# Attention scores as three products of 64 rows, for the two halves of each head pair side by side

## The chip, the cores and the metric

One core of one Trainium2 chip. The metric is the device time of one execution in microseconds. An engine runs its own instructions in the order in which the program lists them: TensorE multiplies matrices into PSUM banks, VectorE and ScalarE work elementwise, and SyncE's queue issues most DMA transfers.

## The reference

Two layers over 256 latent and 256 context tokens of width 2048, in float32. The first layer mixes by a long convolution and a state space model. The second, which the change is in, is differential attention: 16 heads, and each has two halves of 64 channels with a softmax of their own.

```python
q_l = rope_2d(rms_norm(qk_shape(q_l, n_lat), q_norm))   # 16 heads, 2 halves, 64 channels
k_l = rope_2d(rms_norm(qk_shape(k_l, n_lat), k_norm))
...
s = jnp.einsum('bqhmd,bkhmd->bhmqk', q, k) * (DA_HEAD ** -0.5)
p = jax.nn.softmax(s, axis=-1)
w = p[:, :, 0] - lam * p[:, :, 1]
return jnp.einsum('bhqk,bkhe->bqhe', w, v)
```

The last layer makes queries for the 256 latent tokens only; keys and values come from all 512 tokens.

## The kernel before

Products that need precision are made from a high and a low part of each operand in fp32r: the cast (ScalarE) gives the high part, a subtraction (VectorE) the low one. A projection adds three products, high by high, high by low and low by high (lines 108 to 110). Its weights come through SyncE in pieces of 128x1024, three deep (`weights`), and are split the same way (lines 174 and 175).

The second layer runs over four chunks `c` of four heads. For each chunk:

- `project_rows` makes the queries (two token tiles), the keys (four) and the values (four). It goes over the 16 blocks of the inner dimension in pieces of two, and in each piece over up to four PSUM banks: two of the tag `acc` and two of the tag `aux`. Every tag has two banks.
- `heads` takes one finished bank of queries or keys: it norms (lines 1154 to 1160, at high priority; line 1160 is the last to read the bank), scales and rotates (1163 to 1173), transposes four times into a bank of the tag `tp` (1177), and calls `dst`, which is `queries` or `keys`. Then channels stand in rows: 64 rows for the first half of the head, 64 for the second.
- `keys` stacks for each half the high part in that half's own 64 rows and the low part in the other 64 (lines 1186 and 1187). `queries` puts the high part into both groups of 64 rows of one tile, and the low part into both of another (lines 1197 and 1199). So one product over 128 rows gives high by high plus high by low, and a second one the two with the low part of the query.
- For each head and each of two query tiles of 128 tokens: for each half `m`, a bank of the tag `wk`, two products of 128 rows and 512 columns (line 1259), the maximum (1260) and the exponential (1262), which is the last to read the bank. Then the weights are combined and transposed (1270, 1271), and later multiplied with the values into another `wk` bank (1277), normed (line 1283 is the last to read that bank) and transposed (1284). A projection for the gate (line 1248) comes ahead of each head; steps of the last gates (`last_gates`, products of 128 rows and 32 columns in line 580) come behind it.

The order of the instructions on each engine is not the order of the code. A planner goes through the program with costs of its own: an engine takes, of the instructions that are ready in the planner's time, the one that stands first in the code (or has high priority). An instruction that touches a new tile is ready once a buffer of its tag is free. So TensorE has products of the next projection between those of a head. The order is then fixed, and on the chip each engine waits at its semaphores in that order.

Names in the trace: `k` and `q` are the key and query tiles, `ps_wk`, `ps_acc`, `ps_aux` and `ps_tp` the banks, `prob` the weights, `s5HG`, `s5W`, `s5T` and `s5U` tiles of the first layer, where products of 64 rows and 64 columns (line 483) stand beside products of 128 rows and 64 columns (line 479).

Of the kernel before, what the change touches and what calls it, by code (L numbers as in the profile page):

```python
# [10 lines left out]
F32 = mybir.dt.float32  # L11
F32R = mybir.dt.float32r
# [3 lines left out]
MULT, ADD, SUB = ALU.mult, ALU.add, ALU.subtract  # L16
# [479 lines left out]
def hybrid_kernel(ctx: ExitStack, tc: tile.TileContext, A, out):  # L496
    nc = tc.nc
    v, act, pe, dma = nc.vector, nc.scalar, nc.tensor, nc.sync
# [3 lines left out]
    k = K(tc, main, psum)  # L502
# [194 lines left out]
    def project_rows(W, col, h, toks, done):  # L697
        bs = [k.bank("acc" if i < 2 else "aux") for i in range(len(toks))]
        rows(W, col, h, toks, bs, 0, len(h))
        for b, t in zip(bs, toks):  # L700
            done(t, b)
# [46 lines left out]
    W_in = A["ev_in_w"][0]  # L748
# [26 lines left out]
    with phase("start"):  # L775
# [13 lines left out]
        for i, w in enumerate((w1, w2)):  # L789
            b = k.bank("wk")  # L790
            pe.matmul(b[:64, :256], w, prev, start=True, stop=True)
            z = k.t([64, 256], "hyz")
# [33 lines left out]
        x = x_tiles()  # L826
# [56 lines left out]
        h = []  # L883
# [266 lines left out]
    def heads(i, tl, b, dst, t0):  # L1150

        with tc.high_priority():
            sq = k.e([128, 512], "qt", bufs=QT)
            act.activation(sq, b, AF.Square)
            r = k.e([128, 8], "qr", bufs=2)
            v.tensor_reduce(r, sq.rearrange("p (h j) -> p h j", h=8), axis=mybir.AxisListType.X, op=ADD)
            v.tensor_scalar(r, r, 1.0 / 64.0, EPS, op0=MULT, op1=ADD)
            r = rsqrt(k, r, [128, 8], "qrs")
            x = k.e([128, 8, 64], "qt", bufs=QT)
            v.tensor_tensor(x, b.rearrange("p (h j) -> p h j", h=8), r[:, :, None].to_broadcast([128, 8, 64]), op=MULT)  # L1160
        y = k.e([128, 8, 64], "qt", bufs=QT)
        if tl is None:
            v.tensor_tensor(y, x, nw[:, i][:, None, :].to_broadcast([128, 8, 64]), op=MULT)
        else:
            v.tensor_tensor(y, x, tab[:, i, 0, tl][:, None, :].to_broadcast([128, 8, 64]), op=MULT)
            z = sq.rearrange("p (h j) -> p h j", h=8)
            z4, x4 = (a.rearrange("p h (a z j) -> p (h a) z j", a=2, z=2) for a in (z, x))
            s4 = tab[:, i, 1, tl].rearrange("p (a z j) -> p a z j", a=2, z=2)
            for e in range(2):
                v.tensor_tensor(z.rearrange("p h (a z j) -> p h a z j", a=2, z=2)[:, :, :, e],  # L1170
                                x.rearrange("p h (a z j) -> p h a z j", a=2, z=2)[:, :, :, 1 - e],
                                s4[:, :, e][:, None].to_broadcast([128, 8, 2, 16]), op=MULT)
            v.tensor_tensor(y, y, z, op=ADD)
        tb = k.bank("tp", [128, 4, 128])
        yf = y.rearrange("p h j -> p (h j)")
        for c in range(4):
            pe.transpose(tb[:, c], yf[:, c * 128:c * 128 + 128], ident)
        dst(tb, t0)

    def keys(K):  # L1180

        def put(tb, t0):
            for m in range(2):
                s, o = slice(64 * m, 64 * m + 64), slice(64 - 64 * m, 128 - 64 * m)
                hi = K[m][s, :, t0:t0 + 128]
                act.copy(hi, tb[s])
                v.tensor_tensor(K[m][o, :, t0:t0 + 128], tb[s], hi.bitcast(F32), op=SUB)
        return put

    def queries(Q):  # L1190

        def put(tb, t0):
            for m in range(2):
                s, o = slice(64 * m, 64 * m + 64), slice(64 - 64 * m, 128 - 64 * m)
                hi, lo = (Q[m][z][:, :, t0:t0 + 128] for z in range(2))
                for p in (s, o):
                    act.copy(hi[p], tb[s])
                for p in (s, o):
                    v.tensor_tensor(lo[p], tb[s], hi[s].bitcast(F32), op=SUB)
        return put  # L1200

    with phase("mix"):
# [34 lines left out]
    with phase("attention"):  # L1237
        hl = [x[1] for x in h]
        om = []
        for c in range(4):  # L1240
            kT = [k.t([128, 4, 512], n, F32R) for n in ("k0", "k1")]
            qT = [[f([128, 4, 256], f"q{m}{z}", F32R) for z in range(2)] for m, f in enumerate((k.e, k.t))]
            vt = k.t([128, 4, 512], "vt", bufs=1)
            project_rows(W_in, c * 512, h, (2, 3), lambda t, b: heads(0, t - 2, b, queries(qT), (t - 2) * 128))
            project_rows(W_in, 2048 + c * 512, h, range(4), lambda t, b: heads(1, None if t < 2 else t - 2, b, keys(kT), t * 128))
            project_rows(W_in, 4096 + c * 512, h, range(4), lambda t, b: act.copy(vt[:, t], b))
            for hd in range(4):
                b = project(W_in, 6144 + (c * 4 + hd) * 128, hl, 0, 256)
                gt = k.t([128, 256], "gt", bufs=GT)
                act.activation(gt, b[:, :256], AF.Silu)  # L1250
                wT = [k.t([128, 4, 128], "wT", bufs=WT) for _ in range(2)]
                for qt in range(2):
                    z = k.t([128, 2], "z", bufs=4)
                    mx = k.t([128, 2], "mx", bufs=4)
                    ps = []
                    for m in range(2):
                        b = k.bank("wk")
                        for part in range(2):
                            pe.matmul(b, qT[m][part][:, hd, qt * 128:qt * 128 + 128], kT[m][:, hd], start=part == 0, stop=part == 1)  # L1259
                        v.tensor_reduce(mx[:, m:m + 1], b, axis=mybir.AxisListType.X, op=ALU.max, negate=True)  # L1260
                        p = k.t([128, 512], "prob", bufs=4)
                        act.activation(p, b, AF.Exp, bias=mx[:, m:m + 1], accum_out=z[:, m:m + 1])
                        ps.append(p)
                    v.reciprocal(z, z)
                    v.tensor_scalar(z[:, 1:2], z[:, 1:2], nlam, None, op0=MULT)
                    v.tensor_scalar(ps[0], ps[0], z[:, 0:1], None, op0=MULT)
                    v.scalar_tensor_tensor(ps[0], ps[1], z[:, 1:2], ps[0], op0=MULT, op1=ADD)
                    tb = k.bank("tp", [128, 4, 128])
                    for t in range(4):
                        pe.transpose(tb[:, t], ps[0][:, t * 128:t * 128 + 128], ident)  # L1270
                    act.copy(wT[qt], tb)
                ob = k.bank("tp")
                for qt in range(2):
                    qs = slice(qt * 128, qt * 128 + 128)
                    b = k.bank("wk")
                    for t in range(4):
                        pe.matmul(b[:, :128], wT[qt][:, t], vt[:, t, hd * 128:hd * 128 + 128], start=t == 0, stop=t == 3)  # L1277
                    o2 = k.t([128, 128], "o2", bufs=2)
                    r = k.t([128, 1], "or", bufs=2)
                    act.activation(o2, b[:, :128], AF.Square, accum_out=r)  # L1280
                    v.tensor_scalar(r, r, 1.0 / 128.0, EPS, op0=MULT, op1=ADD)
                    r = rsqrt(k, r, [128, 1], "ors")
                    v.tensor_scalar(o2, b[:, :128], r, None, op0=MULT)
                    pe.transpose(ob[:, qs], o2, ident)
                o = k.t([128, 256], "og", bufs=2)
                v.scalar_tensor_tensor(o, ob[:, :256], sw, gt, op0=MULT, op1=MULT)
                om.append([None, halves(o, k.m, "hlo")])
                next(rest)

        def residual(n, t, b):  # L1290
            g, xt = gate(1, 0, n, "prob", 4), k.t([128, 512], "prob", bufs=4)
            dma.dma_start(xt, x1scr[t - 2, n])
            v.tensor_tensor(g, b, g, op=MULT)
            v.tensor_tensor(g, g, xt, op=ADD)
            dma.dma_start(out[0, t * 128 - 256:t * 128 - 128, n * 512:n * 512 + 512], g)

        run(rest)
        W_out = A["od_out_w"][0]
        for n0 in (0, 2):
            bs = [[k.bank(tag) for _ in range(2)] for tag in ("acc", "aux")]  # L1300
            for k0, k1 in ((0, 12), (12, 16)) if n0 == 0 else ((0, 16),):
                for i in range(2):
                    rows(W_out, (n0 + i) * 512, om, (2, 3), bs[i], k0, k1)
                    if k1 == 16:
                        for j in range(2):
                            residual(n0 + i, 2 + j, bs[i][j])
# [29 lines left out]
```

## Time and profile before

| what | value |
|---|---|
| median of 3 runs | 1941.38 us (1938.76 to 1941.87) |
| the profiled execution | 1941.88 us |
| its span | 1939.7 us |
| TensorE busy | 1856.1 us (96%), 12607 products |
| weight loads busy | 1463.5 us (75%) |
| VectorE busy | 1286.6 us (66%) |
| ScalarE busy | 794.5 us (41%) |
| mean HBM traffic | 179 GB/s |

The span is the time from the first to the last instruction on the chip. PE is TensorE's products, PEld its weight loads, DVE is VectorE and ACT is ScalarE. The ends of products are modelled, and products overlap: the pace of a row of products is read from their starts. The attention stage runs from about 1215 us; scores are made in four stretches, 1310 to 1379, 1474 to 1543, 1638 to 1707 and 1802 to 1875 us.

### The profile page before, as it was taken

What the parts mean: (1) busy time and instruction counts of PE and PEld (TensorE: products, weight loads), DVE (VectorE), ACT (ScalarE), POOL (GpSimd) and SP (SyncE); (2) the same over time, 40 slices, a digit from 0 to 9 for tenths busy, and PEclk for the clock granted to TensorE, in tenths of its full rate; (3) what the DMA queues carried; (4) which work ended last, traced back from release to release, by engine and by line L of the source; (5) the groups of instructions that cost most, each with busy time, mean ns of one, the idle gap of its engine ahead of it and who ended that gap; (6) DMA issues with size and microseconds to landing.
All of it is one profiled execution on the core that took longest, in us unless ns stands there. A gap on an engine that the chain in (4) does not pass through costs nothing.

```text
span 1939.7 us, 31835 instructions
## 1 busy us (share of the span) xinstructions
PE 1856.1 (96%) x12607; PEld 1463.5 (75%) x12607; DVE 1286.6 (66%) x2497; ACT 794.5 (41%) x1252; POOL 6.9 (0%) x23
## 2 busy tenths in 40 slices
PE   3799989999999999999999999999999999999999
PEld 2677767777777677777788887778878878887877
DVE  3876677998997477368564347656765864666675
ACT  2442232322332333223342247437636734753762
POOL 0000000000000000000000000000000000000000
PEclk9899999999999999999999999999999999999999
DMA  8877656576774577655656355336335325523557
GB/s 268 273 247 263 206 177 206 176 214 215 226 227 126 177 257 249 209 179 179 227 180 204 119 164 163 89 109 186 106 109 175 108 87 156 168 90 109 181 168 239
DMA packets 325637, 349.63 MB, mean 180 GB/s; under 512 B 53424, under 2 KB 204530, under 8 KB 325490
## 3 DMA queue, kind: packets, MB, share of 16 engines
q1 hardware_dynamic: 314208, 339.86, 55.7%
q10 hardware_dynamic: 10850, 5.93, 1.2%
q8 instruction: 99, 1.62, 0.3%
q0 software_dynamic: 432, 1.84, 0.3%
q14 instruction: 48, 0.39, 0.1%
HBM read 316.07 MB, written 31.49 MB: 179 GB/s over the span
## 4 chain that ended last, share of the span: by engine, by line
PE 66%; DVE 7%; DMA 6%; issue 2%; ACT 2%; SPq 0%; ACTq 0%; DVEq 0%
PE ps_acc L108 13%; PE ps_acc L110 13%; PE ps_acc L109 13%; PE ps_aux L108 5%; PE ps_aux L110 5%; PE ps_aux L109 5%; DMA gw<-in_mod_w_dram 4%; PE ps_aux L580 3%; PE ps_wk L1259 2%; DVE wlo L175 1%; PE ps_wk L1277 1%; DVE s5st L425 1%; PE ps_wk L108 1%; ACT whi L174 1%; PE ps_wk L399 1%
## 5 line engine op out<-in xcount | busy, mean ns | idle before, releaser
L175 DVE TENSOR_TENSOR wlo<-raw,whi 128x1024 fp32r<-128x1024 f32 x304 | 371.0, 1222 | 341.8 <-ACT whi L174 337.6
L174 ACT CAST whi<-raw 128x1024 fp32r<-128x1024 f32 x304 | 319.0, 1049 | 641.8 <-PE ps_acc L109 303.4
L108 PE MATMUL ps_acc<-hhi,whi 128*128 128x512 f32 x768 | 312.0, 407 | 0.4 <-DVE hf L929 0.3
L109 PE MATMUL ps_acc<-hlo,whi 128*128 128x512 f32 x768 | 308.0, 401 | 0.0
L110 PE MATMUL ps_acc<-hhi,wlo 128*128 128x512 f32 x768 | 307.8, 401 | 0.0
L108 PEld LDWEIGHTS ps_acc<-hhi,whi 128*128 128x128 f32 x768 | 144.5, 189 | 42.7 <-issue 10.1
L110 PEld LDWEIGHTS ps_acc<-hhi,wlo 128*128 128x128 f32 x768 | 144.9, 189 | 35.0 <-issue 2.5
L109 PEld LDWEIGHTS ps_acc<-hlo,whi 128*128 128x128 f32 x768 | 145.0, 189 | 34.4 <-issue 3.6
L108 PE MATMUL ps_acc<-whi,hhi 128*128 128x512 f32 x416 | 165.4, 398 | 1.5 <-DVE qt L1160 0.9
L109 PE MATMUL ps_acc<-wlo,hhi 128*128 128x512 f32 x416 | 163.6, 393 | 0.0
L580 PE MATMUL ps_aux<-gw,cst 128*32 128x128 f32 x2048 | 90.9, 288 | 30.4 <-DMA gw<-in_mod_w_dram 26.1
L580 PEld LDWEIGHTS ps_aux<-gw,cst 128*32 128x32 f32 x2048 | 57.4, 113 | 65.1 <-DMA gw<-in_mod_w_dram 36.0
L108 PE MATMUL ps_aux<-whi,h 128*128 128x512 f32 x256 | 100.4, 395 | 4.8 <-DVE qt L1160 4.8
L109 PE MATMUL ps_aux<-wlo,h 128*128 128x512 f32 x256 | 101.6, 397 | 0.0
L110 PE MATMUL ps_aux<-whi,h 128*128 128x512 f32 x256 | 101.3, 396 | 0.0
L110 PE MATMUL ps_acc<-whi,hhi 128*128 128x512 f32 x256 | 101.0, 394 | 0.0
L108 PEld LDWEIGHTS ps_acc<-whi,hhi 128*128 128x128 f32 x416 | 78.2, 188 | 22.8 <-DVE qt L1160 3.9
L109 PEld LDWEIGHTS ps_acc<-wlo,hhi 128*128 128x128 f32 x416 | 78.2, 188 | 16.0
L110 PE MATMUL ps_acc<-whi,hlo 128*128 128x512 f32 x224 | 88.4, 394 | 0.0
L108 PE MATMUL ps_acc<-h,whi 128*128 128x256 f32 x256 | 72.5, 283 | 0.0
L110 PE MATMUL ps_acc<-h,wlo 128*128 128x256 f32 x256 | 71.6, 280 | 0.0
L109 PE MATMUL ps_acc<-h,whi 128*128 128x256 f32 x256 | 71.3, 278 | 0.0
(413 smaller groups left out, 3473.5 us busy)
## 6 DMA issues: line engine op xcount, KB each, us to landing
gw<-in_mod_w_dram SPq DMA_DIRECT2D x128, 512.0 KB
raw<-in_od_in_w_dram SPq DMA_DIRECT2D x128, 512.0 KB
raw<-in_ev_in_w_dram SPq DMA_DIRECT2D x96, 512.0 KB
raw<-in_ev_out_w_dram SPq DMA_DIRECT2D x40, 512.0 KB
hhi<-in_mod_w_dram SPq DMA_DIRECT2D x64, 256.0 KB
qt<-in_mod_w_dram SPq DMA_DIRECT2D x64, 256.0 KB
raw<-in_od_out_w_dram SPq DMA_DIRECT2D x32, 512.0 KB
spill_hp<-out SPq DMA_DIRECT2D x24, 256.0 KB
```

Of the source, the lines that this page charges most:

```text
L108: nc.tensor.matmul(out, lh, rh, start=start, stop=False)
L109: nc.tensor.matmul(out, lh, rl, start=False, stop=False)
L110: nc.tensor.matmul(out, ll, rh, start=False, stop=stop)
L174: k.nc.scalar.copy(hi, src)
L175: k.nc.vector.tensor_tensor(lo, src, hi.bitcast(F32), op=SUB)
L399: nc.tensor.matmul(wb[64 * h:64 * h + 64, r, j], HT[:, r, j, 64 * h:64 * h + 64], U[:, h * 4 + j], start=True, stop=True)
L425: eng.tensor_tensor(t, Lh.rearrange("p a d r g -> p a d (r g)"), at(cf, cb, True), op=MULT)
L580: pe.matmul(b[32 * q:32 * q + 32, :128], cst[:, kk], w[:, q * 128:q * 128 + 128], start=kk == first, stop=kk == last)
L1259: pe.matmul(b, qT[m][part][:, hd, qt * 128:qt * 128 + 128], kT[m][:, hd], start=part == 0, stop=part == 1)
L1277: pe.matmul(b[:, :128], wT[qt][:, t], vt[:, t, hd * 128:hd * 128 + 128], start=t == 0, stop=t == 3)
```

## The change

The high parts of both halves of a head go into one tile and the low parts into another, for queries and for keys alike: one cast and one subtraction over 128 rows for each token tile, by the new function `parts`. There are no copies into the other half's rows. A query tile of a head takes both `wk` banks first. Then for high by high, low by high and high by low it issues one product of 64 rows for each half, the first half in rows 0 to 63 and the second in rows 64 to 127, each into its own bank. The maxima and exponentials follow behind all six products. The query tiles take 8 KB less of each partition (two tiles in place of four).

```diff
-    def keys(K):
+    def parts(X):
         def put(tb, t0):
-            for m in range(2):
-                s, o = slice(64 * m, 64 * m + 64), slice(64 - 64 * m, 128 - 64 * m)
-                hi = K[m][s, :, t0:t0 + 128]
-                act.copy(hi, tb[s])
-                v.tensor_tensor(K[m][o, :, t0:t0 + 128], tb[s], hi.bitcast(F32), op=SUB)
-        return put
-    def queries(Q):
-        def put(tb, t0):
-            for m in range(2):
-                s, o = slice(64 * m, 64 * m + 64), slice(64 - 64 * m, 128 - 64 * m)
-                hi, lo = (Q[m][z][:, :, t0:t0 + 128] for z in range(2))
-                for p in (s, o):
-                    act.copy(hi[p], tb[s])
-                for p in (s, o):
-                    v.tensor_tensor(lo[p], tb[s], hi[s].bitcast(F32), op=SUB)
+            hi, lo = (x[:, :, t0:t0 + 128] for x in X)
+            act.copy(hi, tb)
+            v.tensor_tensor(lo, tb, hi.bitcast(F32), op=SUB)
         return put
...
-            qT = [[f([128, 4, 256], f"q{m}{z}", F32R) for z in range(2)] for m, f in enumerate((k.e, k.t))]
+            qT = [k.e([128, 4, 256], n, F32R) for n in ("q0", "q1")]
...
-                    for m in range(2):
-                        b = k.bank("wk")
-                        for part in range(2):
-                            pe.matmul(b, qT[m][part][:, hd, qt * 128:qt * 128 + 128], kT[m][:, hd], start=part == 0, stop=part == 1)
+                    bs = [k.bank("wk") for _ in range(2)]
+                    for i, (x, y) in enumerate(((0, 0), (1, 0), (0, 1))):
+                        for m, b in enumerate(bs):
+                            s = slice(64 * m, 64 * m + 64)
+                            pe.matmul(b, qT[x][s, hd, qt * 128:qt * 128 + 128], kT[y][s, hd], start=i == 0, stop=i == 2)
+                    for m, b in enumerate(bs):
                         v.tensor_reduce(mx[:, m:m + 1], b, axis=mybir.AxisListType.X, op=ALU.max, negate=True)
```

The two calls of `heads` pass `parts(qT)` and `parts(kT)`. Everything else is as before.

## Rows read from the trace of the kernel before

**Rows 1.** Busy us (instructions) by stretch; then clock, DMA share, GB/s.
```profile
1310.00:1379.00 69.00, 68.50 (x517) 57.55 (x516) 50.14 (x121) 55.18 (x99) 0.00 (x0) 1.00 0.56 171
...
sum 725.00, PE 712.44 PEld 585.65 DVE 453.59 ACT 383.85 POOL 0.00; mean PE 79.16 PEld 65.07 DVE 50.40 ACT 42.65 POOL 0.00
```
**Rows 2.** Waits of TensorE, 1215 to 1940 us: total us, times, longest.
```profile
PE ps_aux L108 <- DVE qt L1160: 4.8, 4, 1.2
```
**Rows 3.** Timeline of TensorE, merged: start us, length us, instruction, count.
```profile
1369.11 0.62 PE L1259 MATMUL ps_wk<-k,q 128*128 128x512 f32 x2
1369.57 0.39 PE L108 MATMUL ps_acc<-whi,h 128*128 128x512 f32 x1
```
**Rows 4.** Timeline of TensorE in the S5 output of the first layer.
```profile
498.63 0.28 PE L483 MATMUL ps_wk<-s5HG,s5W 64*64 64x128 f32 x2
498.65 0.28 PE L483 MATMUL ps_tp<-s5HG,s5W 64*64 64x128 f32 x2
498.85 0.32 PE L479 MATMUL ps_wk<-s5T,s5U 128*64 128x128 f32 x1
...
499.22 0.38 PE L483 MATMUL ps_wk<-s5HG,s5W 64*64 64x128 f32 x2
...
499.44 0.28 PE L483 MATMUL ps_wk<-s5HG,s5W 64*64 64x128 f32 x2
...
499.55 0.28 PE L483 MATMUL ps_wk<-s5HG,s5W 64*64 64x128 f32 x2
```
**Rows 5.** Timeline of TensorE where scores border on the gates' products.
```profile
1310.18 1.09 PE L1259 MATMUL ps_wk<-k,q 128*128 128x512 f32 x4
1311.20 1.08 PE L580 MATMUL ps_aux<-qt,cst 128*32 128x128 f32 x32
...
1331.07 0.85 PE L580 MATMUL ps_aux<-qt,cst 128*32 128x128 f32 x20
1331.85 0.74 PE L1259 MATMUL ps_wk<-k,q 128*128 128x512 f32 x2
1332.42 0.28 PE L108 MATMUL ps_acc<-h,whi 128*128 128x256 f32 x1
```
**Rows 6.** Timeline of TensorE, the two banks of two query tiles.
```profile
1315.16 0.74 PE L1259 MATMUL ps_wk<-k,q 128*128 128x512 f32 x2
...
1315.97 0.63 PE L1259 MATMUL ps_wk<-k,q 128*128 128x512 f32 x2
...
1346.46 0.71 PE L1259 MATMUL ps_wk<-k,q 128*128 128x512 f32 x2
...
1348.42 0.70 PE L1259 MATMUL ps_wk<-k,q 128*128 128x512 f32 x2
```
**Rows 7.** Timeline of TensorE, start of a value projection.
```profile
1256.64 0.45 PE L108 MATMUL ps_acc<-whi,hhi 128*128 128x512 f32 x1
...
1261.60 0.50 PE L108 MATMUL ps_acc<-whi,hhi 128*128 128x512 f32 x1
...
1266.14 0.40 PE L110 MATMUL ps_acc<-whi,hhi 128*128 128x512 f32 x1
1267.74 0.47 PE L108 MATMUL ps_aux<-whi,h 128*128 128x512 f32 x1 [1.21 <-DVE qt L1160]
```
**Rows 8.** Groups by form, 1215 to 1940 us: busy us, mean ns.
```profile
L1187 DVE TENSOR_TENSOR k<-ps_tp,k 64x512 fp32r<-64x512 f32 x32 | 22.0, 688 | 3.4 <-ACT k L1186 2.5
L1259 PEld LDWEIGHTS ps_wk<-k,q 128*128 128x128 f32 x128 | 21.3, 195 | 3.8 <-ACT prob L1262 1.5 <-issue 0.8
L1186 ACT CAST k<-ps_tp 64x512 fp32r<-64x512 f32 x32 | 18.5, 579 | 31.8 <-PE ps_tp L1177 18.8 <-DVE k L1187 12.9
```
**Rows 9.** Timeline of VectorE ahead of the third bank's release.
```profile
1264.42 0.68 DVE L1187 TENSOR_TENSOR k<-ps_tp,k 64x512 fp32r<-64x512 f32 x1 [0.62 <-ACT k L1186]
...
1265.98 0.69 DVE L1187 TENSOR_TENSOR k<-ps_tp,k 64x512 fp32r<-64x512 f32 x1
...
1266.91 0.69 DVE L1160 TENSOR_TENSOR qt<-ps_aux,qrsy 128x512 f32<-128x512 f32 x1
```

More of the change, by code (lines that the diff above doesn't have):

```diff
@@ L1241, in hybrid_kernel @@
             kT = [k.t([128, 4, 512], n, F32R) for n in ("k0", "k1")]
-            qT = [[f([128, 4, 256], f"q{m}{z}", F32R) for z in range(2)] for m, f in enumerate((k.e, k.t))]
+            qT = [k.e([128, 4, 256], n, F32R) for n in ("q0", "q1")]
             vt = k.t([128, 4, 512], "vt", bufs=1)
-            project_rows(W_in, c * 512, h, (2, 3), lambda t, b: heads(0, t - 2, b, queries(qT), (t - 2) * 128))
-            project_rows(W_in, 2048 + c * 512, h, range(4), lambda t, b: heads(1, None if t < 2 else t - 2, b, keys(kT), t * 128))
+            project_rows(W_in, c * 512, h, (2, 3), lambda t, b: heads(0, t - 2, b, parts(qT), (t - 2) * 128))
+            project_rows(W_in, 2048 + c * 512, h, range(4), lambda t, b: heads(1, None if t < 2 else t - 2, b, parts(kT), t * 128))
             project_rows(W_in, 4096 + c * 512, h, range(4), lambda t, b: act.copy(vt[:, t], b))
```

## The prediction

> **What bounds the kernel now.** I read the busy time by stage first, then the waits of TensorE in the attention, then the order of its products and of its neighbours. From 1215 us to the end TensorE is busy for 712.4 of 725 us; while scores are made (1310 to 1379 us is one of four such stretches) for 68.50 of 69 us, with VectorE at 50 and ScalarE at 55 us and the full clock granted [rows 1]. So TensorE's queue is the limit there: what it gains or loses reaches the end, and work taken off the other engines pays only where TensorE waits for it. It has one such wait in each chunk of four heads: the projection of the values can't start on its third bank until VectorE has read the keys out of it, 4.8 us in four waits [rows 2].
>
> A score product costs TensorE what its issue takes, not its recorded length. Two take 0.46 us from the first's start to that of the next instruction, 0.23 us each, though a record is about 0.39 us long and overlaps the next [rows 3]. A query tile of a head has four of them, 0.92 us, and there are 32 query tiles (4 chunks, 4 heads, 2 tiles).
>
> **The products.** Four products of 128 rows become six of 64 rows. A product still streams 512 columns, so I price each at 0.23 us. Two that use different halves of the rows and write different banks can run at once: in the S5 output, products on two row halves into two banks start 0.02 us apart, and a new group of such products starts every 0.11 us [rows 4]. Side by side the six take 3 x 0.23 = 0.69 us, 0.23 us less than now; one after another 1.38 us, 0.46 us more.
>
> **Going to half rows and back.** The neighbours of the scores use all 128 rows. The trace has no change from 128*128 to 64*128, so I take the nearest. From 64*64 to 128*64, only the rows change: the next start comes 0.20 us after the last (498.65 to 498.85) where groups follow at 0.11, so 0.09 us is lost, and on the way back the first group lasts 0.22 us (499.22 to 499.44) in place of 0.11: 0.11 us more [rows 4]. Score products beside the 128*32 products of the gates say the same: four and the change take 1.02 us in place of 0.92, and two right after the change 0.57 in place of 0.46 [rows 5]. I take 0.20 us a change, 0.40 us for a visit to half rows. The bounds are 0.10 (only one of the two halves is lost) and 0.25 us.
>
> So a query tile whose six products stay together, alternating, costs 0.69 + 0.40 - 0.92 = +0.17 us: the overlap gains less than the two changes cost.
>
> **Do they stay together?** This decides the sum. The two score banks of a tile come free one after the other, since the bank of the first half is released by its own exponential or its own output row, and the second bank later. In the trace only one tile in each chunk (as at 1310.18 [rows 5]) has its four products in a row. In one per chunk two other products stand between the two banks' pairs, their first products 0.81 us apart; in the other six there are 6 to 28 others, as between 1346.46 and 1348.42, 1.96 us apart (1.83 to 3.66 in all) [rows 6]. The new code asks for alternation only by the order in which it is written. The planner doesn't hold back for that: at the start of the value projection, the code goes through four banks for each piece of weights, but 18 products, three pieces' worth, run into the first bank before the second gets its first at 1261.60, and 18 more into that one up to 1266.14, while the third is still taken [rows 7]. By the same rule the first half's three products go as soon as its bank is free, in 0.69 us, then other products of 128 rows, then the second half's three, alone. The overlap is lost, and there are two visits to half rows:
>
> - 24 tiles (six a chunk) split: 6 x 0.23 + 4 x 0.20 - 0.92 = 1.26 us each, 30.2 us.
> - 4 tiles with 0.81 us between: I take five steps and one visit, 1.15 + 0.40 - 0.92 = 0.63 us each, 2.5 us (0.17 to 1.26 are the ends).
> - 4 tiles together: 0.17 us each, 0.7 us.
> - In three places a chunk, 12 in all, scores border on the 128*32 products as at 1310.18 and on both sides of 1331.07 to 1331.85 [rows 5]: a change is paid there today, so one of the new ones is not extra, -2.4 us.
>
> That is +31.0 us on TensorE.
>
> The loads of the stationary half stay hidden, as I price it. A load lasts 195 ns beside products at 0.23 us [rows 8], on the same rows. The Trainium skill (TensorE: Matmul & The Clock Gate, Part 3, "The mechanism") says that a weight load overlaps running products only if it goes to another row group. The rows here don't bear that out for full rows; if it held for a run of three products on one half, each further product would show its load as after a change. That is the fourth rival below.
>
> **Splitting into high and low parts.** 64 casts of 64 rows (two for each of 16 key tiles, four for each of 8 query tiles) become 24 of 128 rows, and 64 subtractions likewise; a row count has no price, as 128x512 casts and subtractions are paid by their 512 columns. So 40 x 0.58 = 23 us leave ScalarE and 40 x 0.69 = 28 us leave VectorE [rows 8]. TensorE doesn't wait for these, but for what stands behind them: in the wait of each chunk VectorE runs a subtraction of the keys (1265.98, 0.69 us) shortly before the read that frees the third bank (1266.91), and another at 1264.42 [rows 9]. The product follows 1.60 us after the one before it (1266.14 to 1267.74 [rows 7]), 1.37 us over its pace. One subtraction less in that stretch gives back 0.69 us, two end the wait: 4 x 0.69 = 2.8 to 4 x 1.37 = 5.5 us. I take the middle, -4.1 us; the other end, from a re-sorted VectorE queue with other work before that read, is as much the other way, +5.5 us. What is late next is the weight pieces of the value projection, which are three deep and already on chip by then. The smaller query tiles in memory and the second half's bank being asked for earlier cost nothing by themselves: the first touch of a bank is what waits. The maxima of the first half wait for a third product, 0.23 us more, covered by the projection's products that fill TensorE there.
>
> **Sum.** +31.0 - 4.1 = +26.9 us. The profiled execution took 1941.88 us (span 1939.7, and 2.2 around it), 0.5 above the median of the runs shown: 1941.9 + 26.9 = 1968.8 us.
>
> **Rivals.**
> 1. The products stay together in all tiles, and a change costs 0.20 us. For it: the code asks for both banks before the first product. Against it: [rows 6, 7]. 32 x 0.17 - 2.4 - 4.1 = -1.1: 1940.8 us, no change.
> 2. Not slower, but faster: together in all tiles, and the changes cost nothing from these neighbours, which are of the same column width (128) and type, unlike those of [rows 4, 5]. 32 x (-0.23) - 4.1 = -11.5: 1930.4 us. It decides by the price of one change: under 0.115 us (0.23 / 2) a tile kept together gains. It needs nearly all tiles together: already with two split tiles at the measured price rival 1 is back at the time before.
> 3. It doesn't do what it says: the products alternate, but the two halves run one after another on the chip. 32 x (1.38 + 0.40 - 0.92) - 2.4 - 4.1 = +21.0: 1962.9 us. Against it: the 0.02 us in [rows 4].
> 4. Split as forecast, and the loads show: in 24 tiles four products each pay 0.11 us more, +10.6 us: 1979.4 us. Against it: the hidden loads of [rows 8].
>
> **How the numbers follow.** Forecast 0.64; rivals 0.12, 0.10, 0.07, 0.07. The forecast's own range is 1957 (112 changes at 0.10 us, and the whole wait gone) to 1980 us (no relief on VectorE, no change saved, and the four middle tiles split). For 8 in 10 the range goes down to rival 1 and up past rival 4: 1938 to 1982; it leaves out rival 2 and the far ends. A difference under 0.2%, 3.9 us, can't be told from none by this measurement. Faster: rival 2 and the low side of rival 1, 0.12; same: the rest of rival 1, 0.10; slower: 0.78.
>
> **What would show it.** In the profile after: score products in runs of three of one bank with 128-row products between, about 0.23 us apart within a run; starts 0.3 us after a score run and a first step of 0.34 us; 192 products that take some 60 us with their changes in place of 30; the wait for the third bank in the value projection at 0 to 0.7 us a chunk; 24 casts and 24 subtractions. It is wrong if the six products of most tiles stand together, if changes cost under 0.1 us, or if TensorE's idle time in the attention moves by more than 5 us.

## The result and the profile after

The changed kernel takes 1963.16 us (median of four runs, 1960.48 to 1967.69) where the kernel before takes 1940.66 us (four runs, 1938.76 to 1941.87): a ratio of 1.0125, with a 95% interval of 1.0104 to 1.0146. Slower by 22.5 us; the forecast was 26.9 us slower, and its mechanism is the one that the trace shows. The profiled execution took 1962.52 us, 20.6 more than the one before.

The page's first part, against the table of before:

```profile
span 1960.4 us, 31872 instructions
...
PE 1881.4 (96%) x12671; PEld 1468.6 (75%) x12671; DVE 1263.0 (64%) x2457; ACT 774.7 (40%) x1214; POOL 6.9 (0%) x23
```

TensorE has 64 products more (192 scores in place of 128), VectorE and ScalarE have 40 and 38 instructions less (ScalarE has 40 casts less and two loads of its function table more). The same stretches as in [rows 1], with the same columns:

```profile
1310.00:1379.00 69.00, 68.50 (x466) 53.23 (x465) 46.45 (x114) 52.84 (x96) 0.00 (x0) 1.00 0.48 149
1215.00:1960.40 745.40, 737.70 (x4166) 590.57 (x4164) 428.86 (x902) 361.94 (x589) 0.00 (x0) 1.00 0.43 135
```

TensorE is as full as before, at the same clock. VectorE has 24.7 us and ScalarE 21.9 us less to do in the attention, and the time doesn't show it: the queue of TensorE has 25.3 us more.

The attention repeats with each chunk, so its pace is read from the first scores of the first and the fourth chunk. After:

```profile
1306.36 0.96 PE L1246 MATMUL ps_wk<-k,q 64*128 64x512 f32 x6
1307.24 1.08 PE L580 MATMUL ps_aux<-qt,cst 128*32 128x128 f32 x32
...
1815.65 0.96 PE L1246 MATMUL ps_wk<-k,q 64*128 64x512 f32 x6
```

Before, the first chunk's is in [rows 5], at 1310.18, and the fourth's is:

```profile
1802.58 1.09 PE L1259 MATMUL ps_wk<-k,q 128*128 128x512 f32 x4
```

A chunk takes (1815.65 - 1306.36) / 3 = 169.76 us in place of (1802.58 - 1310.18) / 3 = 164.13: +5.63 us, 22.5 us for four. So the whole loss is in the attention. The profiled pair shows 2 us less because the attention of the changed kernel began 2.1 us earlier in its run; from 1031 to 1218 us of the run before, ahead of anything that was changed, the same products all start 2.1 to 2.2 us earlier.

Where TensorE's time went in the first chunk is a sum of steps, from the start of each product to the start of the next, sorted by what the product is (worked out from the timelines):

| us in the first chunk | before | after | difference |
|---|---|---|---|
| scores | 8.30 | 12.29 | +3.99 |
| products of 256 columns (gate projection) | 23.21 | 24.82 | +1.61 |
| transposes of the outputs | 0.59 | 1.28 | +0.69 |
| products with the values | 6.80 | 7.34 | +0.54 |
| products of 512 columns (projections) | 114.73 | 113.76 | -0.97 |
| the rest | 10.32 | 10.28 | -0.04 |
| sum | 163.95 | 169.77 | +5.82 |

Of the 6.8 us added in the upper four rows 2.8 stand at the neighbours of the scores, which are unchanged instructions. That is what a change of rows looks like: the step of the product ahead of it is longer, and so is that of the first one behind it. A run of three, in the timeline of TensorE:

```profile
1322.61 0.27 PE L1272 MATMUL ps_tp<-ident,o 128*128 128x128 f32 x1
1322.81 0.96 PE L1246 MATMUL ps_wk<-k,q 64*128 64x512 f32 x3
1323.70 0.38 PE L108 MATMUL ps_acc<-h,whi 128*128 128x256 f32 x1
1323.92 0.29 PE L109 MATMUL ps_acc<-h,whi 128*128 128x256 f32 x1
```

The transpose's step is 0.20 us where transposes follow each other at 0.11 us, the three scores take 0.89 us in place of 3 x 0.23 = 0.69, and the product behind them 0.22 us in place of 0.11 to 0.12. That is 0.09 + 0.20 + 0.10 = 0.39 us for the visit.

The new instructions by form (busy us, mean ns, then idle time ahead of them), and the waits of TensorE from 1215 us on (us, times, longest):

```profile
L1246 PE MATMUL ps_wk<-k,q 64*128 64x512 f32 x192 | 52.8, 426 | 1.7 <-ACT prob L1250 1.7
L1246 PEld LDWEIGHTS ps_wk<-k,q 64*128 64x128 f32 x192 | 27.0, 184 | 16.2 <-issue 5.9 <-ACT prob L1250 4.2 <-ACT hlo L651 1.4
L1185 DVE TENSOR_TENSOR k<-ps_tp,k 128x512 fp32r<-128x512 f32 x16 | 10.8, 676 | 2.7 <-ACT k L1184 2.5
L1184 ACT CAST k<-ps_tp 128x512 fp32r<-128x512 f32 x16 | 9.3, 580 | 20.9 <-PE ps_tp L1177 20.9
```

```profile
PE ps_wk L1246 <- ACT prob L1250: 1.7, 8, 0.2
PE ps_acc L108 <- DVE qt L1160: 0.9, 1, 0.9
```

A cast or subtraction of 128 rows costs what one of 64 rows did (580 and 676 ns against 579 and 688 in [rows 8]). The wait of [rows 2] is gone from the list; in its place the first products of two score runs a chunk wait for a bank that an exponential still reads, 1.7 us in all. At the start of the value projection the third bank now comes in time:

```profile
1263.44 0.39 PE L109 MATMUL ps_acc<-wlo,hhi 128*128 128x512 f32 x1
1263.77 0.47 PE L108 MATMUL ps_aux<-whi,h 128*128 128x512 f32 x1
```

The step is 0.33 us and there is no idle time, where it was 1.60 in [rows 7]: 1.27 us a chunk are back, 5.1 us for four. On VectorE one subtraction stands ahead of the read that frees that bank, where [rows 9] have two:

```profile
1261.29 0.69 DVE L1185 TENSOR_TENSOR k<-ps_tp,k 128x512 fp32r<-128x512 f32 x1 [0.64 <-ACT k L1184]
...
1262.93 0.69 DVE L1160 TENSOR_TENSOR qt<-ps_aux,qrsy 128x512 f32<-128x512 f32 x1
```

One thing in the order was not foreseen. Six scores stand in a row between the two query tiles of the third head:

```profile
1347.85 0.27 PE L1272 MATMUL ps_tp<-ident,o 128*128 128x128 f32 x1
1348.05 0.53 PE L1246 MATMUL ps_wk<-k,q 64*128 64x512 f32 x2
...
1348.05 0.98 PE L1246 MATMUL ps_wk<-k,q 64*128 64x512 f32 x6
1348.97 0.50 PE L108 MATMUL ps_acc<-whi,h 128*128 128x512 f32 x1
```

The second row is the answer for the 0.2 us from 1348.00, the third that for the whole run. The six are not one tile: they are the second half of the first query tile and the first half of the second one, whose banks came free together. They stand in the queue as three of the one half and then three of the other. Yet two start 0.03 us apart, where products of one half are 0.23 us apart or more, and all six take 0.92 us, three steps and the change.

### The profile page after: what moved, and what is told of

It reads as the page before. It is cut to its first block, busy times and chain, and to the rows that moved or that the text cites. A ratio compares the mean times of both kernels' runs of the same rounds, so it can differ in the third digit from the quotient of the medians.

```text
span 1960.4 us, 31872 instructions
## 1 busy us (share of the span) xinstructions
PE 1881.4 (96%) x12671; PEld 1468.6 (75%) x12671; DVE 1263.0 (64%) x2457; ACT 774.7 (40%) x1214; POOL 6.9 (0%) x23
## 5 line engine op out<-in xcount | busy, mean ns | idle before, releaser
L108 PE MATMUL ps_acc<-hhi,whi 128*128 128x512 f32 x768 | 312.8, 408 | 0.4 <-DVE hf L929 0.2
L108 PEld LDWEIGHTS ps_acc<-hhi,whi 128*128 128x128 f32 x768 | 144.9, 189 | 42.8 <-issue 9.7
L108 PE MATMUL ps_acc<-whi,hhi 128*128 128x512 f32 x416 | 164.7, 396 | 1.2 <-DVE qt L1160 0.9
L108 PE MATMUL ps_aux<-whi,h 128*128 128x512 f32 x256 | 101.0, 395 | 0.0
L108 PEld LDWEIGHTS ps_acc<-whi,hhi 128*128 128x128 f32 x416 | 78.2, 188 | 21.1 <-DVE qt L1160 2.7
L108 PE MATMUL ps_acc<-h,whi 128*128 128x256 f32 x256 | 74.6, 291 | 0.0
```

What stands on the lines that cost most here:

```text
L108: nc.tensor.matmul(out, lh, rh, start=start, stop=False)
```

## The experiments

The theory: the loss comes from the splitting of the tiles, which loses the overlap of the halves and adds visits, and from 0.20 us for each change of rows. Against it stand above all the prediction's rivals 2 (the changes cost nothing) and 3 (the halves run one after the other on the chip); each expectation names its own. Ratios are to the kernel before on the same chip, with the 95% interval.

**Held together.** The changed kernel with edges for the planner alone (no semaphore): a tile's six products form a chain, and its first one stands behind the reciprocal of the tile before, or behind the last transpose of the head before, when the planner has both banks free.

```diff
+                            mm = pe.matmul(b, qT[x][s, hd, qt * 128:qt * 128 + 128], kT[y][s, hd], start=i == 0, stop=i == 2)
+                            if mms:
+                                behind(mms[-1], mm)
+                            elif free:
+                                behind(free[-1], mm)
+                            mms.append(mm)
...
-                    v.reciprocal(z, z)
+                    free.append(v.reciprocal(z, z))
...
-                    pe.transpose(ob[:, qs], o2, ident)
+                    free.append(pe.transpose(ob[:, qs], o2, ident))
```

> The changed kernel, with edges for the planner alone: the first score product of a query tile stands on TensorE behind what frees the second bank, and the six products stand in a row, alternating between the halves, in all 32 tiles. Theory (the order costs the time: separate visits to half rows at 0.40 us each and the lost overlap): 32 x (0.69 + 0.40 - 0.92) = +5.4 us, -0.8 for four borders with the gates' products, -5.5 for the wait in the value projections that is gone: about 1940 us, ratio to before 0.997 to 1.003. Rival (192 products and their weight loads in place of 128 cost the time, in whatever order they stand): no change against the changed kernel, 1963 us, ratio 1.012.

Measured: 1943.81 us, ratio 1.002 [1.0003, 1.0037]. All 32 tiles have their six in a row:

```profile
1349.48 0.97 PE L1252 MATMUL ps_wk<-k,q 64*128 64x512 f32 x6
1350.38 0.50 PE L110 MATMUL ps_acc<-whi,h 128*128 128x512 f32 x1
```

So 1.05% of the 1.25% is given back by the order of the same instructions: the splitting of the tiles is the loss. But even with every tile kept together the change gains nothing, since 0.90 us for six and the late neighbours on both sides (0.20) are 0.18 more than the 0.92 us of four full products. In one tile of each chunk (as at 1306.64) the second bank comes late on the chip, its half starts 0.26 us behind the first, and the six take 1.16 us. Waiting for both banks has a price too, ahead of the transposes of the weights:

```profile
PE ps_tp L1269 <- DVE prob L1266: 4.1, 8, 0.6
```

**The six products over 128 rows**, in the order of the changed kernel (so the two halves of a head are mixed in the scores): no change of rows, no overlap.

```diff
-    s = slice(64 * m, 64 * m + 64)
+    s = slice(0, 128)
```

> The changed kernel with its six score products over all 128 rows in place of 64 (the halves of a head are mixed in the scores, so its output is not the reference's); TensorE's order is that of the changed kernel, instruction by instruction. No product runs beside another and no change of rows is paid. Theory (steps and changes): 48 steps a chunk of 0.23 us against 32, +14.7 us, -5.5 for the wait that is gone: +9.2, about 1950 us, ratio 1.005. Of the changed kernel's cost the changes are then some 18 us and the missing overlap the rest. Rival (a change of rows costs nothing from these neighbours; the cost is unpaired products): 41 steps become 48, +6.4 us over the changed kernel, about 1969 us, ratio 1.015.

Measured: 1951.52 us, 1.0049 [1.0021, 1.0078]. The changed kernel is 0.76% above this one, 14.7 us. My terms for that difference: 52 visits at 0.40 us less 12 changes paid anyway at 0.20 is 18.4 us, less 7 steps a chunk that overlap saves (48 against 41), 28 x 0.23 = 6.4: 12.0 us. The intervals leave some 8 to 22 us for the difference of the two ratios; the pace of the chunks is the closer measure: (1813.10 - 1312.50) / 3 = 166.87 us here against 169.76, 11.6 us for four. A run of three behind the same transpose shows the visit itself:

```profile
1328.88 0.27 PE L1272 MATMUL ps_tp<-ident,o 128*128 128x128 f32 x1
1328.91 0.93 PE L1246 MATMUL ps_wk<-k,q 128*128 128x512 f32 x3
1329.68 0.28 PE L108 MATMUL ps_acc<-h,whi 128*128 128x256 f32 x1
1329.80 0.28 PE L109 MATMUL ps_acc<-h,whi 128*128 128x256 f32 x1
```

From the transpose to the second product behind the run it is 0.92 us, where the changed kernel takes 1.31 at 1322.61: 0.39 us. The price of changing rows is measured here with the number and the order of the products held: the changes are not free, and they are more than the overlap that is left gives back.

**The new splitting alone.** The changed kernel's two tiles for high and low parts with four products of 128 rows as before (halves mixed again).

```diff
-    for i, (x, y) in enumerate(((0, 0), (1, 0), (0, 1))):
-        for m, b in enumerate(bs): ... # six products of 64 rows
+    for part in range(2):
+        pe.matmul(b, qT[part][:, hd, ...], kT[m][:, hd], start=part == 0, stop=part == 1)
```

> The changed kernel's splitting (one cast and one subtraction of 128 rows) with four score products of 128 rows as before (two for each bank, by the high and the low part of the query; the halves of a head are mixed, so its output is not the reference's). Theory: the splitting alone ends the wait for the third bank of the value projections, 4 x 1.37 = 5.5 us: 1935 us, ratio 0.997. Rival (the freed time on ScalarE and VectorE is off the path and the wait only moves): no change, ratio 1.000.

Measured: 1931.94 us, 0.9959 [0.9937, 0.9981], 8 us faster (4 to 12), where the theory had 5.5 from the wait alone. The pace agrees: (1799.69 - 1313.30) / 3 = 162.13 us, 2.00 less a chunk. The waits of TensorE from 1205 us on have no row for the third bank:

```profile
PE ps_acc L108 <- DVE qt L1160: 0.8, 1, 0.8
PE ps_tp L1259 <- DVE prob L1256: 0.6, 4, 0.2
```

In the first chunk the projections' products of 512 columns take 1.88 us less than before: 1.3 are the wait, and most of the rest is that 22 of their steps are about 0.3 us long where 27 were. Why there are fewer no run shows. So one part of the change was a gain, and the other used it up.

**By halves.** The kernel held together, with the queue's order changed: the first half's three products, then the second half's three.

```diff
-    for i, (x, y) in enumerate(((0, 0), (1, 0), (0, 1))):
-        for m, b in enumerate(bs):
+    for m, b in enumerate(bs):
+        for i, (x, y) in enumerate(((0, 0), (1, 0), (0, 1))):
```

> As the run with the six products in a row, but in the queue the first half's three stand ahead of the second half's three. Theory in its strict form (TensorE starts products in the order of its queue, so that only the third of the first half and the first of the second run side by side): five steps in place of three, 32 x 0.46 = +14.7 us over that run, about 1955 us, ratio 1.007. Rival (products of the two halves run beside each other however they are queued, as six at 1348.05 us in the changed kernel's trace seem to: starts 0.03 us apart in twos): the same as that run, about 1940 us, ratio 1.000.

Measured: 1944.51 us, 1.002 [1.0005, 1.0036], the same as alternating. In the timeline, again the answer for 0.2 us ahead of that for the run:

```profile
1346.59 0.33 PE L1283 MATMUL ps_tp<-ident,o 128*128 128x128 f32 x1
1346.85 0.51 PE L1252 MATMUL ps_wk<-k,q 64*128 64x512 f32 x2
...
1346.85 0.97 PE L1252 MATMUL ps_wk<-k,q 64*128 64x512 f32 x6
1347.75 0.51 PE L108 MATMUL ps_acc<-whi,h 128*128 128x512 f32 x1
```

Two start at once (0.01 us apart) though the queue has three of one half first; so it is in 24 of the 32 tiles. In the other eight the second half starts later (by 0.16 us as at 1330.86, or 0.60 us as at 1310.73). My theory of a strict order within the queue was wrong and the rival right. What costs the overlap is other products between the halves, or a second half that can't start yet, and not their order.

**One visit for a head.** Held together, with the twelve products of both query tiles in a row, the second tile's scores in the two `tp` banks: half as many changes.

```diff
+    sc = [[k.bank(tag) for _ in range(2)] for tag in ("wk", "tp")]
+    for qt in range(2):
+        ... # the six products of this tile into sc[qt], chained behind the ones before
```

> One visit to half rows for each head: all twelve score products of its two query tiles in a row, alternating between the halves, the second tile's scores in the two tp banks, held on TensorE behind what ends the head before. Theory (a visit costs 0.40 us, and the splitting with 128 rows gives 8 us as the run of it alone measured): 16 x (1.38 + 0.40 - 1.84) = -1 us on the products, -8 from the splitting: about 1931 us, ratio 0.996, where the run with a visit for each tile had 1.002. Rival (the four banks come together so late that TensorE runs out of other products and waits for the softmax of each head): its idle time in the four stretches grows by several us, 1944 us or more, ratio 1.002 or more.

Measured: 1943.22 us, 1.0023 [1.0005, 1.0041], and not the 1931 us of the theory. The visit does what it should, twelve products in 1.60 us, which is 6 x 0.23 and 0.22:

```profile
1305.93 0.97 PE L1249 MATMUL ps_wk<-k,q 64*128 64x512 f32 x6
1306.74 0.86 PE L1249 MATMUL ps_tp<-k,q 64*128 64x512 f32 x6
1307.53 1.08 PE L580 MATMUL ps_aux<-qt,cst 128*32 128x128 f32 x32
```

What it saves, 16 visits at 0.40 us or 6.4 us, is lost in waits: the transposes of the weights need a `tp` bank, and that is free only when the second tile's exponential has read it.

```profile
PE ps_tp L1269 <- DVE prob L1266: 9.2, 12, 0.9
PE ps_tp L1269 <- DVE z L1263: 4.3, 4, 1.1
```

These are 13.5 us against 4.1 when tiles are held one by one. The rival that named this wait was right.

**The kernel before, held together**: its four products of a tile chained by the same edges. It tells what the holding costs by itself.

```diff
+                    last = free[-1] if free else None
...
+                            mm = pe.matmul(b, qT[m][part][:, hd, qt * 128:qt * 128 + 128], kT[m][:, hd], start=part == 0, stop=part == 1)
+                            if last:
+                                behind(last, mm)
+                            last = mm
```

> The kernel before, with edges for the planner alone: the four products of 128 rows of a query tile stand in a row behind what frees the second bank, as in the run with the six together. Theory (holding has a price of its own: in that run TensorE waits 0.8, 0.9 and 0.5 us in each chunk ahead of transposes of the weights and outputs): 4 us or so more than before, 1944 us, ratio 1.002. Rival (holding is free, other products fill in): no change, ratio 1.000.

Measured: 1942.17 us, 1.0021 [1.0005, 1.0038], 4 us slower (1 to 7), the size that my theory had. Its cause is another: the waits ahead of the transposes of the weights, which the theory named, are 1.1 us in all against 0.7 before. The wait for the third bank is unchanged (`PE ps_aux L108`), and the holding cuts the gates' products into eight runs in the first chunk where there were six, as here between the transposes and the products with the values:

```profile
PE ps_aux L108 <- DVE qt L1160: 4.8, 4, 1.2
```

```profile
1313.14 0.63 PE L1279 MATMUL ps_tp<-ident,prob 128*128 128x128 f32 x4 [0.27 <-DVE prob L1276]
1313.70 1.06 PE L580 MATMUL ps_aux<-qt,cst 128*32 128x128 f32 x26
1314.69 1.16 PE L1286 MATMUL ps_wk<-vt,wT 128*128 128x128 f32 x8
1315.78 0.42 PE L580 MATMUL ps_aux<-qt,cst 128*32 128x128 f32 x6
```

Their steps in that chunk are 5.67 us against 4.76; the chunk is longer by the same 0.91 us, and the other classes' small differences cancel. The next two chunks are longer by 0.60 and 0.13 us, so this is the dearest of them.

**Later subtractions.** The kernel before, with the keys' subtractions of token tiles 0 and 1 issued behind `rd`, the read that frees the third bank. Nothing is taken away, only moved.

```diff
+        if i == 1 and t0 == 256:
+            with tc.issue_after(rd.ins):
+                while held:
+                    v.tensor_tensor(*held.pop(0), op=SUB)
...
-                v.tensor_tensor(K[m][o, :, t0:t0 + 128], tb[s], hi.bitcast(F32), op=SUB)
+                held.append((K[m][o, :, t0:t0 + 128], tb[s], hi.bitcast(F32)))
+            while held and t0 > 128:
+                v.tensor_tensor(*held.pop(0), op=SUB)
```

> The kernel before, with one edit of order: the four key subtractions of token tiles 0 and 1 stand on VectorE behind the read that frees the third bank of the value projection (edges for the planner, the arithmetic is the same). Theory (the changed splitting helped by clearing VectorE's queue ahead of that read, and by nothing else): the wait of 1.4 us a chunk ends, 4 x 1.37 = -5.5 us, ratio 0.997, and the chunk's period falls from 164.1 us to about 162.7. Rival (the wait moves to the fourth bank or into the keys, since the four subtractions now stand ahead of token tile 3): the period stays above 163.5 us, ratio 0.999 to 1.001.

Measured: 1936.29 us, 0.9994 [0.998, 1.0009]: not told from no change. A chunk takes 163.65 us, where the theory had 162.7 and the rival more than 163.5. The wait is neither gone nor the same:

```profile
PE ps_aux L108 <- DVE qt L1162: 3.9, 8, 0.8
```

Four waits of up to 1.2 us became eight of up to 0.8: the subtractions now stand ahead of the read that frees the fourth bank. The rival was mostly right.

**Later still.** The same with the subtractions of token tiles 0 to 2 behind the read of the fourth bank.

```diff
-        if i == 1 and t0 == 256:
+        if i == 1 and t0 == 384:
...
-            while held and t0 > 128:
+            while held and t0 > 256:
```

> As the run with the key subtractions of tiles 0 and 1 behind the read of tile 2's bank, but the subtractions of tiles 0 to 2 stand behind the read of tile 3's bank, the last that the value projection needs. Theory (the wait is VectorE's queue ahead of the reads of the third and the fourth bank): both waits end, the period of a chunk falls from 164.1 us to about 162.5, ratio 0.997. Rival (the reads are bound by their own chain of square, root and scale, not by the subtractions): the period stays at 163.6 us as in that run, ratio 0.999.

Measured: 1936.35 us, 0.9973 [0.9955, 0.999]. Both banks come nearly in time:

```profile
PE ps_tp L1183 <- DVE qt L1179: 1.1, 4, 0.3
PE ps_acc L108 <- DVE qt L1162: 0.8, 1, 0.8
PE ps_aux L108 <- DVE qt L1162: 0.7, 4, 0.2
```

The wait of 4.8 us is 0.7, with 1.1 new at the transposes; 5.2 us faster (2 to 9), and a chunk takes 162.97 us, 1.16 less than before. So VectorE's subtractions ahead of the banks' reads were the cause of the wait, as the relief in the forecast supposed. This version keeps the products of before and is faster than both kernels.

## Why the prediction was right

The forecast was the case in which the two halves of a tile are split, and the time of 1963.16 us lies in its own range (1957 to 1980). Step by step:

- **TensorE is the bound.** Right. The removal of 40 casts and 40 subtractions takes 24.7 and 21.9 us off VectorE and ScalarE, and was worth 8 us by itself, of which some 5 are what TensorE waited for them.
- **The price of a product and of a change.** Right: 0.23 us within runs (0.89 us for three with the change), 0.39 us for a visit where 0.40 was taken from products of another shape in [rows 4, 5].
- **The tiles split.** Right in kind, priced too high. The forecast had 24 split tiles, four with five steps, and four together: 44 steps and 14 visits a chunk. The trace has 41 and 13. The tile with five steps and the one together are as forecast (the latter alternates at 1306.36, 0.88 us for six). The difference is the six at 1348.05: in one head of four, the second half of one tile and the first half of the next meet and run side by side, so 9 steps and 3 visits stand where 12 and 4 were forecast. By the same working: (41 - 32) x 4 x 0.23 + 52 x 0.40 - 2.4 = +26.7 us in place of +31.0. This is the step that was mis-sized: the prediction took it that a half-tile on its own meets only 128-row products.
- **Loads stay hidden.** Right: steps within a run of three on one half are 0.23 us. Rival 4 falls.
- **The relief.** Forecast -4.1 us within 2.8 to 5.5; the step at the third bank fell from 1.60 to 0.33 us, 4 x 1.27 = -5.1 us, near the upper end.
- **What was priced at nothing.** The waits of two score runs a chunk for a bank that an exponential still reads are 1.7 us. The prediction had named the earlier request for the second bank, and the later maxima, and gave both no price; which of them makes the waits, or whether it is only the new order, no run shows.
- **Sum.** 26.7 - 5.1 + 1.7 = +23.3 us against 22.5 from the pace of the chunks. Two errors, 4.3 us too much for the split tiles and 1.0 too little for the relief, point the same way, and the unpriced wait takes back 1.7; that much of the closeness is luck. The upper end of its range, 1980 us, comes to 1978 by the terms that it names, which changes nothing.
- **The signs of being wrong.** None came, though one was near: TensorE's idle time from 1215 us on fell from 12.6 to 7.7 us, by 4.9 where 5 was the limit.

The rivals: 1 and 2 needed the tiles together, which they are not. Rival 2's free changes are refuted by the visits' 0.39 us and by the six products over 128 rows. Rival 1's price was tried: with all tiles together the kernel is 0.2% slower, 3.9 us, where it had 1.1 us less. Of the 5 us between, the waits at the weights' transposes (4.1 us against 0.7 in the kernel before) and the four tiles with a late second bank (1.0 us) are the likely place, but no run took them away: that stays open. Rival 3, the halves in series, had 1962.9 us, the nearest of all to the measured 1963.16; so the time alone decides nothing here, and it is the trace that refutes it, by the pairs that start together.

That the two kernels held together, with half rows (1.002) and with full rows (1.0021), come out the same, though the new splitting into parts gives the first one 5 to 8 us, fits only roughly. On its other side stand 0.18 us for each of 32 tiles, 0.26 more in four of them, and 3.0 us more in waits at the weights' transposes (4.1 against 1.1), less 0.8 for four changes shared with the gates' products: 9.0 us. The 1 to 4 us between are about what these intervals can tell.

## What to carry to other kernels

Two row halves side by side save one product's step for each pair, but each visit to half rows costs two changes, so count the products of one visit: here three pairs save 3 x 0.23 us against the six in series but only 0.23 against four full products, for 0.40 of changes. And before pricing an overlap, ask whether the two partners become ready together: where their buffers are freed one after the other, a planner that takes what is ready separates them. Price the helper work that a change removes apart from its main idea: here the smaller part was worth 8 us by itself.

## What the runs showed of the hardware that was not expected

Two runs of three products on different row halves, in the queue one after the other, start together: all six take 0.90 us, alternating or by halves (1349.48 and 1346.85 in the two kernels held together), and 0.92 across tiles at 1348.05. The opening of this document says that an engine runs its instructions in the order in which the program lists them; for such products it doesn't hold. The Trainium skill (TensorE: Matmul & The Clock Gate, Part 3, "The mechanism") says that products start and end strictly in the order of the program. The trace here differs: at 1346.85 the product that stands fourth in the queue starts 0.01 us behind the first, and the second of the queue 0.34 us behind it.

A change of rows costs on both sides of it, about 0.09 us late for the next start and 0.11 us more for the first step in the new shape. The Trainium skill (TensorEngine Tiling (Array Packing), "Key Properties") says that a change of the tiling mode, and not one of the tile alone, drains TensorE. The trace agrees: there is one price for a visit (0.39 us), and none between the products of the two halves within it (twelve in 1.60 us at 1305.93).
